# A two-layer encoder trunk: 128x128 turns of activations moved from TensorE to VectorE's 32x32 block transpose

## The chip, the cores and the metric

One core of one Trainium2 chip. The metric is the device time of one execution in microseconds (us), as the median of several executions on one chip.

## The reference

An encoder of two layers over 256 tokens of width 2048, all in float32. Each layer does

```
h    = RMSNorm(x)
u    = h @ w_in                       # q, k, v and a gate path z of four attention branches; merge gates
y_n  = attention_n(q, k, v)           # A: windowed, B: 2-D neighbourhood, C: three dilated groups, D: dense
br_n = (y_n * silu(z_n)) @ w_branch_n
m    = sum_n sigmoid(gates_n + gate_b) * br_n
x    = x + m @ w_out
```

and a last RMSNorm closes the trunk. Each branch has 4 query heads of 128.

## The kernel before, in words

**Weights.** All weights stream through the core once, as 640 tiles of 128x1024 float32 (512 KB each), called subs here and numbered j. For accuracy a sub is split in two: ScalarE rounds it to `whi` (L276), VectorE takes the rest, `wlo` = `raw` - `whi` (L277); both lines stand in the helper `halves`. TensorE multiplies the activations' own pair of halves with them, three products for each (L207 to L209 in `mm3`), 12 matmuls of 512 columns for a sub. `raw`, `whi` and `wlo` have four buffers each (`wpool`, L92); `split_w(j + 2)` is written two subs ahead (L693).

**Units.** `unit_list` (L43) sets the order of a layer: units of 8 subs that make 512 columns for all 256 tokens. M units are projections (ck, cv, cq0, cq1, cq2, cz, then akdk, avdv, aq, az, dq, dz, bk, bv, bq, bz), G units merge gates (8 subs), each followed by an R unit (2 subs, the branch's projection), P units the output projection. The order of units is fixed by hand; within an engine the order of instructions is what the tile framework's scheduler makes of it.

**What stands between units.** When a unit's last matmul is done, its 256x512 result lies in PSUM with tokens on partitions. `ev_M` (L304) applies the norm's factor and the rotary angles (`rope`, VectorE, L266 and L271) or the SiLU gate (L318, L319) into the tile `u`. Attention and the next product need features on partitions, so each 512 columns have to be turned: `turn` (L291) turns head by head with TensorE, 128x128 at a time against an identity matrix into PSUM (L299), four turns to a piece; `copy` (L338) or `split` (L346) then moves the piece to SBUF by ScalarE, or by ScalarE and VectorE as halves. `post` is the list of such pieces: one is taken from it after each sub (L704). `ev_branch` (L542) does the same for the merged gates `m` (L559), `ev_out` (L568) for the residual stream `xm`, which becomes the next layer's `h`. `k_pair` (L356) splits the keys of A and D. Attention itself (`attn_slots`, L394) is cut into slots that are spread over the subs behind a branch's z unit (L731).

```
 299   nc.tensor.transpose(tp[:, c, blk * P:(blk + 1) * P], u[:, blk, h * HD:(h + 1) * HD], ident)
 302   post.extend([lambda: None] * 2 + [lambda i=i: f(i) for i in range(n // 2)])
 693   split_w(j + LS)
 701   mm_m(outs[:1] if half else outs, hi, lo, sh, sl, 2 * si, nk, j == 0)
 704   for f in post[:1]:
 705       f()
```

Of the kernel before, what the change touches and what calls it, by code (L numbers as in the profile page):

```python
# [17 lines left out]
P = 128  # L18
SEQ = 256
D = 2048  # L20
# [62 lines left out]
def encoder_kernel(ctx: ExitStack, tc: tile.TileContext, a: dict, out: bass.AP):  # L83
# [17 lines left out]
    def nm(s):  # L101
        uid[0] += 1
        return f"{s}_{uid[0]}"
# [17 lines left out]
    def split_w(j):  # L121
        if j < NSUB:
            raw = raw_q.pop(j)
            hi = wpool.tile([P, 1024], F32R, tag="whi", name=nm("whi"))
            lo = wpool.tile([P, 1024], F32R, tag="wlo", name=nm("wlo"))
            for c in (slice(0, 512), slice(512, 1024)) if j == 0 else (slice(0, 1024),):
                halves(raw[:, c], hi[:, c], lo[:, c])
            wstate[j] = (hi, lo)
# [66 lines left out]

    hs = {}

    def h_split(layer, kt, x):
        t = per.tile([P, 2, SEQ], F32R, tag=f"h{kt}", name=nm("h"))
        g = g_sb[:, layer, kt:kt + 1] if layer else x0[:, kt:kt + 1]  # L200
        halves(x, t[:, 0, :], t[:, 1, :], g)
        hs[kt] = t


    def mm3(o, ah, al, bh, bl, start, stop):
# [24 lines left out]
    def layer_stats(layer, ss):  # L230

        t = sm.tile([P, 2, 2], F32, tag="ssp", name=nm("ssp"))
        v = sm.tile([P, 2], F32, tag="ssv", name=nm("ssv"))
        nc.vector.tensor_tensor(t, ss[:, :, 0:2], ss[:, :, 2:4], op=ALU.add)
        nc.vector.tensor_tensor(v, t[:, :, 0], t[:, :, 1], op=ALU.add)
        nc.vector.tensor_scalar(v, v, 1.0 / D, EPS, ALU.mult, ALU.add)
        S["rc"] = rsqrt(v, 2, "x")
        ev = sm.tile([P, 2], F32, tag="ev", name=nm("ev"))
        nc.vector.tensor_scalar(ev, v, EPS, None, ALU.mult)
        S["ev"] = ev  # L240

    def d_tables(layer, w):

# [44 lines left out]
    def vview(t):  # L288
        return t.rearrange("p a b -> p (a b)").rearrange("p (k m) -> p k m", k=2)

    def turn(u, n, take, post):  # L291


        def f(i):
            tp = ps_tp.tile([P, 2, SEQ], F32, tag="tp", name=nm("tu"))
            for c in range(2):
                for blk in range(2):
                    h = 2 * i + c
                    nc.tensor.transpose(tp[:, c, blk * P:(blk + 1) * P], u[:, blk, h * HD:(h + 1) * HD], ident)  # L299
            take(i, tp)  # L300

        post.extend([lambda: None] * 2 + [lambda i=i: f(i) for i in range(n // 2)])

    def ev_M(layer, name, ps, post):  # L304
        rc = [S["rc"][:, blk:blk + 1] for blk in range(2)]
        x, kind = name[0].upper(), name[1]
        if kind == "v":
            ev_v(ps, {"avdv": "avdv", "bv": "Bv", "cv": "Cv"}[name])
            if x == "B":
                b_mask()  # L310
            return
        u = wk.tile([P, 2, 512], F32, tag="u", name=nm("u"), bufs=1)
        key = x + name[1:]
        for blk in range(2):
            p, o = ps[:, blk, :], u[:, blk, :]
            if kind == "z":
                s = wk.tile([P, 512], F32, tag="t2", name=nm("zs"))
                nc.scalar.activation(s, p, AF.Sigmoid, scale=rc[blk])  # L318
                nc.vector.scalar_tensor_tensor(o, p, rc[blk], s, op0=ALU.mult, op1=ALU.mult)  # L319
            elif x == "B":  # L320
                nc.scalar.activation(o, p, AF.Copy, scale=rc[blk])
            elif x == "C" or name == "aq":
                rope(p, o, blk, cos1, sin1, rc[blk])
            elif name == "akdk":
                rope(p[:, 0:256], o[:, 0:256], blk, cos1, sin1, rc[blk])
                d_squares(p[:, 256:512], 4, blk)
                if blk == 0:
                    S["dku"] = per.tile([P, 2, 256], F32, tag="dku", name=nm("dku"))
                rope(p[:, 256:512], S["dku"][:, blk, :], blk, *S["dt"])
            else:  # L330
                d_squares(p, 0, blk)
                rope(p, o, blk, *S["dt"])
        if name == "akdk":
            turn(u, 2, lambda i, tp: k_pair("A", tp), post)
        elif x == "C" or kind == "z":
            S[key] = st()

            def copy(i, tp):  # L338
                nc.scalar.activation(S[key][:, 2 * i:2 * i + 2, :], tp, AF.Copy,
                                     **({"scale": SCALE} if kind == "q" else {}))  # L340

            turn(u, 4, copy, post)
        else:
            S[key + "h"], S[key + "l"] = st(F32R), st(F32R)

            def split(i, tp):  # L346
                two = slice(2 * i, 2 * i + 2)
                halves(tp, S[key + "h"][:, two, :], S[key + "l"][:, two, :],
                       SCALE if kind == "q" and x != "D" else None)

            if x == "D":
                d_norms()
                turn(S["dku"], 2, lambda i, tp: k_pair("D", tp), post)
            turn(u, 4, split, post)

    def k_pair(x, u):  # L356

        t = st(F32R)
        halves(u, t[:, 0:2, :], t[:, 2:4, :])
        S[x + "kh"], S[x + "kl"] = t[:, 0:2, :], t[:, 2:4, :]  # L360

    def d_squares(p, c, blk):

# [178 lines left out]
    def ev_branch(x, n, ps, post):  # L542
        G = S.pop("G")
        if x == "C":
            S[f"m{n}"] = per.tile([P, 2, 512], F32, tag=f"m{n}", name=nm("m"))
        m = S[f"m{n}"]
        for blk in range(2):
            o = m if x == "C" else G
            nc.vector.tensor_tensor(o[:, blk, :], ps[:, blk, :], G[:, blk, :], op=ALU.mult)  # L549
        if x != "C":  # L550
            nc.vector.tensor_tensor(m, m, G, op=ALU.add)  # L551
        if x == "B":

            def tr(k0):
                def f():
                    tp = ps_tp.tile([P, 2, SEQ], F32, tag="tp", name=nm("mt"))
                    for k in range(2):
                        for blk in range(2):
                            nc.tensor.transpose(tp[:, k, blk * P:(blk + 1) * P],  # L559
                                                m[:, blk, (k0 + k) * P:(k0 + k + 1) * P], ident)  # L560
                    t = st(F32R).rearrange("p (k h) t -> p k h t", k=2)
                    S[f"mt{(4 * n + k0) // 2}"] = t
                    halves(tp, t[:, :, 0, :], t[:, :, 1, :])
                return f
            post.append(tr(0))
            post.append(tr(2))

    def ev_out(n, ps, post):  # L568

        nc.vector.tensor_tensor(xm[n], ps, xm[n], op=ALU.add)  # L570
        for blk in range(2):
            s = squares(F["ss"], n, blk)
        if n == 0:
            sqrt_table(s[:, 0:1])

        def take(i, tp):
            for c in range(2):
                h_split(1, 4 * n + 2 * i + c, tp[:, c, :])

        turn(xm[n], 4, take, post)  # L580

    F = {}

# [54 lines left out]
            squares(F["ss"], n, blk)  # L638

    new_sums()  # L640
    h_tiles(0)
    split_w(0)
    split_w(1)
# [4 lines left out]
             **{8 + n: lambda n=n: first_squares(n) for n in range(4)}}  # L648
    side = []
    post = []  # L650
    last4 = []
    held = []
    j = 0
    for layer in range(DEPTH):
# [3 lines left out]
        for ui, si in sub_list(layer):  # L658
# [3 lines left out]
            if si == 0:  # L662
# [15 lines left out]
                if kind == "R":  # L678
                    yh, yl = S[name + "yh"], S[name + "yl"]
                    sh, sl = (lambda k: yh[:, k, :]), (lambda k: yl[:, k, :])  # L680
                elif kind == "P":
                    sh, sl = (lambda k, h=h: S[f"mt{k // 2}"][:, k % 2, h, :] for h in range(2))
                else:
                    sh, sl = (lambda k, h=h: hs[k][:, h, :] for h in range(2))
                opened[ui] = ps, outs, sh, sl
            ps, outs, sh, sl = opened[ui]
            nk = 2 * nsub
# [9 lines left out]
                layer_stats(0, F["ss"])  # L697
                ev_M(*held.pop())
            hi, lo = wstate.pop(j)
            half = alone and si >= 4  # L700
            mm_m(outs[:1] if half else outs, hi, lo, sh, sl, 2 * si, nk, j == 0)
            if half:
                last4.append((hi, lo, si))
            for f in post[:1]:  # L704
                f()
            del post[:1]
            if si == nsub - 1:
                if kind == "M" and "rc" not in S:
                    held.append((layer, name, ps, post))
                elif kind == "M":  # L710
                    ev_M(layer, name, ps, post)
                elif kind == "G":
                    ev_gate(layer, name, i, ps)
                elif kind == "R":
                    ev_branch(name, i, ps, post)
                elif not final:
                    ev_out(i, ps, post)
                    if i == 3:
                        layer_stats(1, F["ss"])
                else:  # L720
                    ev_last(i, 0, outs[0][1])
                    for h, l, s in last4:
# [133 lines left out]
```

## Time and profile before

| what | value |
|---|---|
| device time, median of 3 | 1867.07 us (1866.35 to 1867.41) |
| profiled execution, its own time | 1866.87 us |
| its span | 1865.1 us (1.8 us lie around it) |
| granted TensorE clock, mean | 0.999 |
| TensorE matmul busy | 1855.1 us, 99% |
| VectorE busy | 1155.6 us, 62% |
| ScalarE busy | 914.8 us, 49% |
| bytes moved by DMA | 356.95 MB, mean 191 GB/s |

The profiled execution stands 0.2 us under the median. Busy time is the time in which at least one instruction of the engine runs. A matmul's duration in the trace includes the part in which the next one already runs, so the step from one matmul's start to the next's (0.227 us for 512 columns) is what counts, not its mean duration.

### The profile page before, as it was taken

How to read it: one execution, taken by the hardware profiler on the slowest of the kernel's cores; microseconds unless marked ns; L12 is line 12 of the kernel's file. 1: busy time of each engine (PE TensorE's matmuls, PEld its weight loads, DVE VectorE, ACT ScalarE, POOL GpSimd, SP SyncE). 2: the span in 40 equal slices, each digit the busy share in tenths (PEclk: the TensorE clock that was granted, in tenths of full speed). 3: DMA queues.
4: the chain of work that ended last, by engine and by line, in shares of the span. 5: the costliest groups of instructions: out<-in, count | busy, mean ns of one | idle time of the engine just before them, and what ended most of it. 6: DMA issues, size and time to landing. Idle time of an engine off the chain costs nothing.

```text
span 1865.1 us, 22697 instructions
## 1 busy us (share of the span) xinstructions
PE 1855.1 (99%) x8560; PEld 1540.4 (83%) x8560; DVE 1155.6 (62%) x1576; ACT 914.8 (49%) x1120; POOL 0.2 (0%) x4
## 2 busy tenths in 40 slices
PE   9999999999999999999999999999999999999998
PEld 7888888888888888888888888888888888888886
DVE  7567675567654755655565576755765547556654
ACT  6445474465444644444544454744654446444443
POOL 0000000000000000000000000000000000000000
PEclk9999999999999999999999999999999999999999
DMA  9655556655765566655555555566567665666654
GB/s 327 195 188 166 170 171 196 203 169 185 219 205 187 159 199 206 200 194 188 185 187 191 182 165 170 173 197 204 174 187 214 201 189 161 204 201 194 219 190 138
DMA packets 110846, 356.95 MB, mean 191 GB/s; under 512 B 19984, under 2 KB 20496, under 8 KB 110736
## 3 DMA queue, kind: packets, MB, share of 16 engines
q1 hardware_dynamic: 110448, 354.98, 59.9%
q8 instruction: 67, 1.10, 0.2%
q10 hardware_dynamic: 288, 0.52, 0.1%
q14 instruction: 43, 0.35, 0.1%
HBM read 353.36 MB, written 2.10 MB: 191 GB/s over the span
## 4 chain that ended last, share of the span: by engine, by line
PE 99%; DMA 0%; DVE 0%; ACT 0%; issue 0%; DVEq 0%; SPq 0%
PE ps L207 31%; PE ps L209 31%; PE ps L208 31%; PE tu L299 1%; PE tp L474 1%; PE mt L559 0%; PE y L209 0%; PE y L207 0%; PE y L208 0%; PE sc L405 0%; PE sc L209 0%; PE sc L208 0%; PE sc L207 0%; PE ps L219 0%; DMA raw<-w 0%; PE sc L407 0%
## 5 line engine op out<-in xcount | busy, mean ns | idle before, releaser
L277 DVE TENSOR_TENSOR wlo<-raw,whi 128x1024 fp32r<-128x1024 f32 (+1 forms) x641 | 782.8, 1222 | 588.9 <-ACT whi L276 586.6
L276 ACT ACTIVATE whi<-raw 128x1024 fp32r<-128x1024 f32 (+1 forms) x641 | 678.4, 1059 | 819.5 <-PE ps L209 765.3
L207 PE MATMUL ps<-whi,h 128*128 128x512 f32 x2044 | 801.9, 392 | 0.0
L209 PE MATMUL ps<-whi,h 128*128 128x512 f32 x2044 | 797.4, 390 | 0.0
L208 PE MATMUL ps<-wlo,h 128*128 128x512 f32 x2044 | 796.7, 390 | 0.0
L209 PEld LDWEIGHTS ps<-whi,h 128*128 128x128 f32 x2044 | 383.7, 188 | 81.0
L208 PEld LDWEIGHTS ps<-wlo,h 128*128 128x128 f32 x2044 | 384.2, 188 | 76.3 <-DVE wlo L277 0.5
L207 PEld LDWEIGHTS ps<-whi,h 128*128 128x128 f32 x2044 | 384.1, 188 | 75.8
L207 PE MATMUL ps<-whi,st 128*128 128x512 f32 x512 | 200.5, 392 | 0.0
L209 PE MATMUL ps<-whi,st 128*128 128x512 f32 x512 | 199.6, 390 | 0.0
L208 PE MATMUL ps<-wlo,st 128*128 128x512 f32 x512 | 199.4, 389 | 0.0
L209 PEld LDWEIGHTS ps<-whi,st 128*128 128x128 f32 x512 | 96.1, 188 | 20.1
L208 PEld LDWEIGHTS ps<-wlo,st 128*128 128x128 f32 x512 | 96.2, 188 | 19.4
L207 PEld LDWEIGHTS ps<-whi,st 128*128 128x128 f32 x512 | 96.2, 188 | 19.4 <-DVE xm L598 0.2
L537 DVE SCALAR_TENSOR_TENSOR G<-ps,ry,gb 128x512 f32<-128x512 f32 x64 | 45.1, 745 | 10.5 <-PE ps L209 10.5
L447 ACT ACTIVATE p<-p,ng 128x256 f32<-128x256 f32 (+1 forms) x48 | 27.7, 578 | 36.9 <-DVE ng L446 28.9
L539 ACT ACTIVATE G<-G 128x1024 f32<-128x1024 f32 x32 | 34.0, 1062 | 10.0 <-DVE G L537 9.9
L549 DVE TENSOR_TENSOR G<-ps,G 128x512 f32<-128x512 f32 x48 | 30.9, 686 | 8.0 <-PE ps L209 8.0
L299 PE MATMUL tu<-tab,u 128*128 128x128 f32 x200 | 30.1, 271 | 0.0
L299 PEld LDWEIGHTS tu<-tab,u 128*128 128x128 f32 x200 | 24.8, 139 | 6.4
L551 DVE TENSOR_TENSOR m<-m,G 128x1024 f32<-128x1024 f32 x24 | 29.2, 1217 | 0.0
L474 PE MATMUL tp<-tab,p 128*128 128x128 f32 x128 | 24.3, 271 | 0.0
(131 smaller groups left out, 790.7 us busy)
## 6 DMA issues: line engine op xcount, KB each, us to landing
raw<-w SPq DMA_DIRECT2D x639, 512.0 KB, 3.8
gb<-gate_b SPq DMA_DIRECT2D x32, 256.0 KB, 4.3
xm<-xm SPq DMA_DIRECT2D x4, 512.0 KB, 8.4
st<-rpb SPq DMA_DIRECT2D x32, 64.0 KB, 4.5
st<-x SPq DMA_DIRECT2D x7, 256.0 KB, 7.1
dx<-tabx SPq DMA_DIRECT2D x4, 256.0 KB, 4.5
st<-fg SPq DMA_DIRECT2D x2, 512.0 KB, 5.3
out<-xm SPq DMA_DIRECT2D x4, 256.0 KB, 2.6
```

Of the source, the lines that this page charges most:

```text
L207: nc.tensor.matmul(o, ah, bh, start=start, stop=False)
L208: nc.tensor.matmul(o, ah, bl, start=False, stop=False)
L209: nc.tensor.matmul(o, al, bh, start=False, stop=stop)
L276: nc.scalar.activation(hi, u, AF.Copy)
L277: nc.vector.tensor_tensor(lo, u, f32(hi), op=ALU.subtract)
L299: nc.tensor.transpose(tp[:, c, blk * P:(blk + 1) * P], u[:, blk, h * HD:(h + 1) * HD], ident)
L447: nc.scalar.activation(p[:, 0:n], p[:, 0:n], AF.Exp, bias=ng, scale=1.0, accum_out=den)
L474: nc.tensor.transpose(H[h][:, k, blk * P:(blk + 1) * P], it["p"][:, k * P:(k + 1) * P], ident)
L537: nc.vector.scalar_tensor_tensor(G[:, blk, :], ps[:, blk, :], S["rc"][:, blk:blk + 1], gb, op0=ALU.mult, op1=ALU.add)
L539: nc.scalar.activation(G, G, AF.Sigmoid)
L549: nc.vector.tensor_tensor(o[:, blk, :], ps[:, blk, :], G[:, blk, :], op=ALU.mult)
L551: nc.vector.tensor_tensor(m, m, G, op=ALU.add)
```

## The change

`turn` now uses VectorE's transpose, which turns blocks of 32x32, for all that TensorE turned before, except the attention weights (L474), which stay on TensorE. One instruction takes 32 partitions `a` to `a+32` and writes them, turned, to partitions `c` to `c+32`, 8 blocks (4 heads, 2 token blocks) of 32 columns at once; 16 of them turn 512 columns, 16 with 4 blocks the 256 columns of a key tile. `post` takes four instructions at a time. Tiles that are wanted whole are written to their place directly (no copy by ScalarE; the scale of the queries is folded into the factor `rcq`); tiles that are wanted as halves go to one buffer `T` and are split from there in one piece of 1024 columns. `whi` and `wlo` have three buffers instead of four, and the last unit's final three subs, not four, are held for its second half.

```
-            hi = wpool.tile([P, 1024], F32R, tag="whi", name=nm("whi"))
-            lo = wpool.tile([P, 1024], F32R, tag="wlo", name=nm("wlo"))
+            hi = wpool.tile([P, 1024], F32R, tag="whi", name=nm("whi"), bufs=3)
+            lo = wpool.tile([P, 1024], F32R, tag="wlo", name=nm("wlo"), bufs=3)
...
+        S["rcq"] = sm.tile([P, 2], F32, tag="rcq", name=nm("rcq"))
+        nc.vector.tensor_scalar(S["rcq"], S["rc"], SCALE, None, ALU.mult)
...
-    def turn(u, n, take, post):
-
-
-        def f(i):
-            tp = ps_tp.tile([P, 2, SEQ], F32, tag="tp", name=nm("tu"))
-            for c in range(2):
-                for blk in range(2):
-                    h = 2 * i + c
-                    nc.tensor.transpose(tp[:, c, blk * P:(blk + 1) * P], u[:, blk, h * HD:(h + 1) * HD], ident)
-            take(i, tp)
-
-        post.extend([lambda: None] * 2 + [lambda i=i: f(i) for i in range(n // 2)])
+    def turn(u, dst, post, done=None):
+
+        x = u.rearrange("p b (h d) -> p h b d", d=HD)
+        y = dst.rearrange("p h (b t) -> p h b t", b=2)
+
+        def f(c):
+            for a in range(0, P, 32):
+                nc.vector.transpose(y[c:c + 32, :, :, a:a + 32], x[a:a + 32, :, :, c:c + 32])
+            if c == 96 and done:
+                done()
+
+        post.extend(lambda c=c: f(c) for c in range(0, P, 32))
...
+    def turned(n=4):
+        return wk.tile([P, 4, SEQ], F32, tag="T", name=nm("T"), bufs=1)[:, 0:n, :]
+
+    def turn_split(u, hi, lo, post):
+        t = turned(hi.shape[1])
+        turn(u, t, post, lambda: halves(t, hi, lo))
...
-            half = alone and si >= 4
+            half = alone and si >= 5
```

Where the turns now stand on VectorE is the scheduler's doing. The first place is the stretch behind a projection of branch C, here unit cq0 of the first layer: `ps` is its result, `u` the rotated tile, `st` the turned one, `wlo` the low halves of the weights that the following subs need. Before, VectorE had there:

```order
L271 TENSOR_TENSOR u_697<-u_697,t_134_698 128x512
L277 TENSOR_TENSOR wlo_732<-raw_679,whi_731 128x1024
L266 SCALAR_TENSOR_TENSOR t_135_703<-ps_552,ry_430,tab 128x4x64 x2
L277 TENSOR_TENSOR wlo_750<-raw_710,whi_749 128x1024
L271 TENSOR_TENSOR u_697<-u_697,t_135_703 128x512
L277 TENSOR_TENSOR wlo_774<-raw_729,whi_773 128x1024
L277 TENSOR_TENSOR wlo_798<-raw_747,whi_797 128x1024
L277 TENSOR_TENSOR wlo_816<-raw_771,whi_815 128x1024
```

and now:

```order
L276 TENSOR_TENSOR u_689<-u_689,t_119_690 128x512
L282 TENSOR_TENSOR wlo_705<-raw_653,whi_704 128x1024
L271 SCALAR_TENSOR_TENSOR t_120_695<-ps_544,rcq_424,tab 128x4x64 x2
L282 TENSOR_TENSOR wlo_728<-raw_671,whi_727 128x1024
L276 TENSOR_TENSOR u_689<-u_689,t_120_695 128x512
L282 TENSOR_TENSOR wlo_750<-raw_702,whi_749 128x1024
L303 STREAM_TRANSPOSE st_700<-u_689 32x8x32 x12
L282 TENSOR_TENSOR wlo_772<-raw_725,whi_771 128x1024
L303 STREAM_TRANSPOSE st_700<-u_689 32x8x32 x4
L282 TENSOR_TENSOR wlo_794<-raw_747,whi_793 128x1024
```

Twelve transposes in a row now stand between two low halves, and four more before the next.

The second place is unit dz and the start of the gate unit behind it, where D's keys (`dku`) and queries are turned through `T` and split (`st`), the gate path is made (`u`) and D's attention begins (`mx`):

```order
L282 TENSOR_TENSOR wlo_3406<-raw_3357,whi_3405 128x1024
L303 STREAM_TRANSPOSE T_3310<-dku_1445 32x4x32 x16
L282 TENSOR_TENSOR wlo_3428<-raw_3379,whi_3427 128x1024
L282 TENSOR_TENSOR st_3309<-T_3310,st_3309 128x512
L282 TENSOR_TENSOR wlo_3450<-raw_3403,whi_3449 128x1024
L303 STREAM_TRANSPOSE T_3311<-u_3275 32x8x32 x12
L282 TENSOR_TENSOR wlo_3472<-raw_3425,whi_3471 128x1024
L303 STREAM_TRANSPOSE T_3311<-u_3275 32x8x32 x4
L282 TENSOR_TENSOR wlo_3511<-raw_3447,whi_3510 128x1024
L324 SCALAR_TENSOR_TENSOR u_3493<-ps_3312,ry_416,zs_3494 128x512
L282 TENSOR_TENSOR st_3293<-T_3311,st_3292 128x1024
L324 SCALAR_TENSOR_TENSOR u_3493<-ps_3312,ry_416,zs_3497 128x512
```

There were only splits of the turned tiles at this place before; now the turns themselves stand there, 16 small and 16 large ones.

## Rows read from the trace of the kernel before

**Rows 1.** The page: busy time of the engines, and the chain that ended last.
```profile
PE 1855.1 (99%) x8560; PEld 1540.4 (83%) x8560; DVE 1155.6 (62%) x1576; ACT 914.8 (49%) x1120; POOL 0.2 (0%) x4
...
PE 99%; DMA 0%; DVE 0%; ACT 0%; issue 0%; DVEq 0%; SPq 0%
```
**Rows 2.** Groups by form, TensorE's turns: count, busy us, mean ns, idle before.
```profile
L299 PE MATMUL tu<-tab,u 128*128 128x128 f32 x200 | 30.1, 271 | 0.0
L559 PE MATMUL mt<-tab,m 128*128 128x128 f32 x64 | 9.8, 276 | 0.1
L299 PE MATMUL tu<-tab,xm 128*128 128x128 f32 x32 | 4.8, 272 | 0.0
L299 PE MATMUL tu<-tab,dku 128*128 128x128 f32 x8 | 1.5, 272 | 0.0
```
**Rows 3.** Timeline, ScalarE, steady stretch of branch C: start us, us, what, idle before.
```profile
94.56 1.06 ACT L276 ACTIVATE whi<-raw 128x1024 fp32r<-128x1024 f32 x1 [1.66 <-PE ps L209]
97.28 1.06 ACT L276 ACTIVATE whi<-raw 128x1024 fp32r<-128x1024 f32 x1 [1.66 <-PE ps L209]
100.00 1.06 ACT L276 ACTIVATE whi<-raw 128x1024 fp32r<-128x1024 f32 x1 [1.66 <-PE ps L209]
```
**Rows 4.** Windows of single units: us, then busy us (count) of each engine.
```profile
74.36:97.09 22.73, 22.73 (x106) 18.80 (x105) 13.80 (x16) 9.47 (x10) 0.00 (x0) 1.00 0.58 186
170.09:197.57 27.48, 27.48 (x142) 23.09 (x141) 22.83 (x58) 13.66 (x24) 0.00 (x0) 1.00 0.48 153
221.29:244.39 23.10, 23.10 (x110) 19.16 (x109) 15.14 (x20) 10.80 (x13) 0.00 (x0) 1.00 0.58 182
383.33:406.92 23.59, 23.59 (x113) 19.53 (x112) 18.06 (x32) 14.07 (x17) 0.00 (x0) 1.00 0.58 182
406.92:435.07 28.15, 28.15 (x152) 23.86 (x151) 20.84 (x47) 21.02 (x35) 0.00 (x0) 1.00 0.50 156
757.79:780.57 22.78, 22.78 (x106) 18.73 (x105) 13.34 (x13) 9.57 (x10) 0.00 (x0) 1.00 0.60 203
```
**Rows 5.** Timeline, VectorE, the same stretch: the rotary part of cq1 between low halves.
```profile
95.65 1.23 DVE L277 TENSOR_TENSOR wlo<-raw,whi 128x1024 fp32r<-128x1024 f32 x1 [1.50 <-ACT whi L276]
97.28 0.75 DVE L266 SCALAR_TENSOR_TENSOR u<-ps,ry,tab 128x512 f32<-128x512 f32 x1 [0.40 <-PE ps L209]
...
99.99 1.22 DVE L277 TENSOR_TENSOR wlo<-raw,whi 128x1024 fp32r<-128x1024 f32 x1
101.12 0.87 DVE L266 SCALAR_TENSOR_TENSOR t<-ps,ry,tab 128x256 f32<-128x256 f32 x2
101.91 1.22 DVE L277 TENSOR_TENSOR wlo<-raw,whi 128x1024 fp32r<-128x1024 f32 x1
103.04 0.68 DVE L271 TENSOR_TENSOR u<-u,t 128x512 f32<-128x512 f32 x1
103.82 1.23 DVE L277 TENSOR_TENSOR wlo<-raw,whi 128x1024 fp32r<-128x1024 f32 x1
```
**Rows 6.** Timeline, TensorE: first matmuls of two subs that use Rows 5's halves.
```profile
97.08 0.39 PE L207 MATMUL ps<-whi,h 128*128 128x512 f32 x1
...
102.52 0.39 PE L207 MATMUL ps<-whi,h 128*128 128x512 f32 x1
```
**Rows 7.** Groups by form, VectorE's nearest operations: count, busy us, mean ns.
```profile
L466 DVE TENSOR_SCALAR p<-p,rd 128x256 f32<-128x256 f32 x64 | 22.5, 352 | 1.7
L271 DVE TENSOR_TENSOR u<-u,t 128x512 f32<-128x512 f32 x24 | 16.4, 682 | 0.0
L277 DVE TENSOR_TENSOR st<-yz,st 128x256 fp32r<-128x256 f32 x32 | 13.4, 420 | 3.0 <-ACT st L276 2.3
L462 DVE TENSOR_TENSOR p<-p 128x128 f32<-128x128 f32 x16 | 4.6, 290 | 9.9 <-ACT p L447 9.9
```
**Rows 8.** Timeline, VectorE: two instructions, the second using the first's result.
```profile
257.36 0.15 DVE L459 TENSOR_TENSOR den<-den,es 128x1 f32<-128x1 f32 x1
257.55 0.16 DVE L465 RECIPROCAL rd<-den 128x1 f32<-128x1 f32 x1
```

More of the change, by code (lines that the diff above doesn't have):

```diff
@@ L196, in encoder_kernel, with h_tile @@
     hs = {}
+    def h_tile(n):
+        hs[n] = per.tile([P, 2, 4, SEQ], F32R, tag=f"h{n}", name=nm("h"))
+        return hs[n]
     def h_split(layer, kt, x):
-        t = per.tile([P, 2, SEQ], F32R, tag=f"h{kt}", name=nm("h"))
+        t = hs[kt // 4][:, :, kt % 4, :]
         g = g_sb[:, layer, kt:kt + 1] if layer else x0[:, kt:kt + 1]
         halves(x, t[:, 0, :], t[:, 1, :], g)
-        hs[kt] = t
     def mm3(o, ah, al, bh, bl, start, stop):
@@ L289, in vview @@
         return t.rearrange("p a b -> p (a b)").rearrange("p (k m) -> p k m", k=2)
-    def turn(u, n, take, post):
-        def f(i):
-            tp = ps_tp.tile([P, 2, SEQ], F32, tag="tp", name=nm("tu"))
-            for c in range(2):
-                for blk in range(2):
-                    h = 2 * i + c
-                    nc.tensor.transpose(tp[:, c, blk * P:(blk + 1) * P], u[:, blk, h * HD:(h + 1) * HD], ident)
-            take(i, tp)
-        post.extend([lambda: None] * 2 + [lambda i=i: f(i) for i in range(n // 2)])
+    def turn(u, dst, post, done=None):
[7 more added lines that the diff above has]
+        post.extend(lambda c=c: f(c) for c in range(0, P, 32))
     def ev_M(layer, name, ps, post):
-        rc = [S["rc"][:, blk:blk + 1] for blk in range(2)]
+        rc = [S["rcq" if name[1] == "q" and name[0] != "d" else "rc"][:, blk:blk + 1] for blk in range(2)]
         x, kind = name[0].upper(), name[1]
@@ L333, in ev_M, with k_pair @@
         if name == "akdk":
-            turn(u, 2, lambda i, tp: k_pair("A", tp), post)
+            k_pair("A", u[:, :, 0:256], post)
         elif x == "C" or kind == "z":
             S[key] = st()
[L338 to L342, printed above, removed]
+            turn(u, S[key], post)
         else:
             S[key + "h"], S[key + "l"] = st(F32R), st(F32R)
[L346 to L349, printed above, removed]
             if x == "D":
                 d_norms()
-                turn(S["dku"], 2, lambda i, tp: k_pair("D", tp), post)
-            turn(u, 4, split, post)
-    def k_pair(x, u):
+                k_pair("D", S["dku"], post)
+            turn_split(u, S[key + "h"], S[key + "l"], post)
+    def turned(n=4):
[3 more added lines that the diff above has]
+        turn(u, t, post, lambda: halves(t, hi, lo))
+    def k_pair(x, u, post):
         t = st(F32R)
-        halves(u, t[:, 0:2, :], t[:, 2:4, :])
         S[x + "kh"], S[x + "kl"] = t[:, 0:2, :], t[:, 2:4, :]
+        turn_split(u, S[x + "kh"], S[x + "kl"], post)
     def d_squares(p, c, blk):
@@ L552, in ev_branch @@
         if x == "B":
[L554 to L566, printed above, removed]
+            S[f"mh{n}"], S[f"ml{n}"] = st(F32R), st(F32R)
+            turn_split(m, S[f"mh{n}"], S[f"ml{n}"], post)
     def ev_out(n, ps, post):
@@ L574, in ev_out, with split @@
             sqrt_table(s[:, 0:1])
[L576 to L580, printed above, removed]
+        h_tile(n)
+        t = turned()
+        def split():
+            for c in range(4):
+                h_split(1, 4 * n + c, t[:, c, :])
+        turn(xm[n], t, post, split)
     F = {}
@@ L640, in encoder_kernel @@
     new_sums()
+    for n in range(4):
+        h_tile(n)
     h_tiles(0)
@@ L650, in encoder_kernel @@
     post = []
-    last4 = []
+    late = []
     held = []
@@ L681, in encoder_kernel @@
                 elif kind == "P":
-                    sh, sl = (lambda k, h=h: S[f"mt{k // 2}"][:, k % 2, h, :] for h in range(2))
+                    sh, sl = (lambda k, h=h: S[f"m{h}{k // 4}"][:, k % 4, :] for h in "hl")
                 else:
-                    sh, sl = (lambda k, h=h: hs[k][:, h, :] for h in range(2))
+                    sh, sl = (lambda k, h=h: hs[k // 4][:, h, k % 4, :] for h in range(2))
                 opened[ui] = ps, outs, sh, sl
@@ L699, in encoder_kernel @@
             hi, lo = wstate.pop(j)
-            half = alone and si >= 4
+            half = alone and si >= 5
             mm_m(outs[:1] if half else outs, hi, lo, sh, sl, 2 * si, nk, j == 0)
             if half:
-                last4.append((hi, lo, si))
+                late.append((hi, lo, si))
             for f in post[:1]:
@@ L721, in encoder_kernel @@
                     ev_last(i, 0, outs[0][1])
-                    for h, l, s in last4:
+                    for h, l, s in late:
                         mm_m(outs[1:], h, l, sh, sl, 2 * s, nk)
```

## The prediction

> **What bounds the kernel now.** I read the page first: TensorE is busy 99% of the span, and the chain that ended last is TensorE's to 99% [rows 1]. So a microsecond taken from TensorE's own work is a microsecond of the whole, and work on VectorE (62% busy) costs only where TensorE comes to wait for it. Next I asked for the groups by form, to count TensorE's turns [rows 2], then for windows of single units, to see what is free on VectorE beside each [rows 4], and for the timelines of one stretch of branch C, to see how far VectorE runs ahead of TensorE [rows 3, 5, 6].
>
> The reader is to see a chain of buffers. ScalarE's rounding of each sub waits until TensorE gives a `whi` buffer back [rows 3]; it comes every 2.72 us, which is one sub. VectorE's low half follows. The low half that ends at 96.88 [rows 5] is used by the sub that starts at 102.52 [rows 6]: it lies 5.64 us ahead. That lead is what VectorE may be late by before TensorE has to wait.
>
> **What the change takes from TensorE.** Rows 2 count 200 + 64 + 32 + 8 = 304 turns, 76 groups of four. A steady unit of eight subs takes 8 x 2.72 = 21.76 us; the first window of rows 4 has two groups in it and takes 22.73. So a group costs 0.97 / 2 = 0.485 us, and 76 of them 36.9 us, all on the path. This is the whole gain; ScalarE's copies that go away were beside TensorE and are counted at nothing.
>
> **What it puts on VectorE.** 36 turns of 16 instructions with 256 columns each (576) and 4 turns of 16 with 128 columns (64). No row shows such an instruction. The nearest are VectorE's operations of the same number of float32 columns between SBUF tiles: 420 ns for 256 columns, 290 ns for 128 [rows 7]. Two instructions that need nothing of each other overlap: in rows 5 the one behind the low half starts at 101.12, though that half ends at 101.21, which is 0.09 us earlier; where the second uses the first's result it starts 0.04 us after the end [rows 8]. So a step of 0.33 us is one end (0.42 - 0.09); below it nothing speaks for a gain, since the transpose has no second input to save. The other end is 0.68 us, the 512-column row of rows 7, if a 4-byte column counts twice. I take **0.46 us** (0.42 + 0.04; for small ones 0.29 + 0.04 = 0.33), because each of these instructions reads other partitions than the one ahead of it, which no overlapping pair of rows 5 does, so I count no overlap.
>
> Beside that row stands a rule. The Trainium skill, "VectorE: DVE Perf Modes", section "Two Vector instructions with no wait between them", says that an instruction which starts in another group of 32 partitions than the last one read or wrote is held until all before it have finished. By that rule the overlap of rows 5 is lost in all 640, and the sum belongs near my value and not near the 0.33 end; no run here shows it yet. The same page, "The three transpose paths", gives 311 ns for 128 bf16 columns; an estimate from it, with 130 ns for 128 more columns by rows 7, is 0.44 us, by which the sum below would be about 1862.
>
> The splits that remain get a little cheaper (one of 1024 columns for two of 512), 0.15 us a turn; I leave that out.
>
> **What the third buffer does.** With three buffers instead of four, a `whi` buffer comes free one sub later, so the lead is at most 5.64 - 2.72 = 2.92 us. In each sub, 2.72 us less the low half's step of 1.13 (99.99 to 101.12, rows 5) leaves 1.59 us for all else; what VectorE does beyond that is taken from the lead, and what goes below zero is time in which TensorE waits.
>
> **Where TensorE then waits**, place by place:
>
> - Branch C's rotated units (three in the first layer, four in the second). The rotary part takes 2.71, 0.79 and 0.78 us between low halves [rows 5], so the lead goes 2.92, 1.80, 2.60, 2.92. Then twelve turns, 5.52 us: 2.92 + 1.59 - 5.52 = -1.01; then four, 1.84: -0.25. That is 1.26 us a unit, 7 units, 8.8 us.
> - The very first unit's 16 turns stand in one run: 2.92 + 1.59 - 7.36 = -2.9 us, once.
> - Unit az, with the turn of A's queries in runs of eight, four and four, the first beside a rotary add and two small operations of 1.3 us in all: 2.60 + 1.59 - 5.0 = -0.8, then twice -0.25. 1.3 us a layer, 2.6.
> - Unit avdv, behind A's and D's keys: VectorE 22.83 + 16 x 0.33 = 28.1 us of work for TensorE's 27.48 - 0.49 = 27.0 [rows 4]; 1.1 us a layer, 2.2.
> - Unit dz and D's first gate unit: VectorE is busy 18.06 + 20.84 = 38.9 us there [rows 4], and gets 16 small and 32 large turns, 5.3 + 14.7: 58.9 us. TensorE needs 23.59 + 28.15 less five groups, 49.3. Of the 9.6 us too much the lead covers 2.92: 6.7 a layer, 13.4 us.
> - All other turns stand by four or six between low halves: 1.84 us against 1.59, four times, which the lead covers. The merged gates' window shows the room: 13.34 + 7.36 = 20.7 us of work in 21.8 [rows 4].
>
> Together 29.9 us. For what these tallies leave out (the scores of D that wait for its queries, the last merged block and the last input block, which TensorE needs within six subs of the layer's turn, ScalarE's rounding that comes late behind a table load) I allow 8 us, an estimate between 0 and 15, since with 2.92 us each of them counts sooner.
>
> **The sum.** 1866.87 - 36.9 + 29.9 + 8 = 1867.9, so **1868 us**; the profiled execution stands 0.2 us under the median, which I neglect. Gain and loss cancel. The one number that decides is the step: 112 turns in C's units, 16 in the first, 96 in D's stretch and 64 around A add up to 288 that stand where nothing covers them, so 10 ns of step are 2.9 us of time.
>
> **The rivals.**
>
> *VectorE overlaps the turns (faster).* If blocks from other partitions step like the pairs of rows 5, at 0.33 us (0.20 for small ones), twelve of them take 3.96 us, under the 4.51 that lead and sub give, and TensorE does not wait in C's units. The first run loses 0.8, D's stretch 38.9 + 3.2 + 10.6 - 49.3 - 2.92 = 0.5 a layer; with half the allowance, 1866.9 - 36.9 + 1.8 + 4 = 1836 us. For it: all independent pairs of rows 5 overlap. Against it: none of them changes partitions. At 0.40 us it is still about 1852. Chance 0.30.
>
> *A 4-byte transpose is slower than an add (slower).* At 0.68 us TensorE waits 3.65 + 1.13 = 4.8 us in a C unit (33 in seven), the first run 6.4, az 4.8 a layer, avdv 2.5, D's stretch 15.2, and the 22 or so turns that were covered lose 4 x 1.13 less the lead, 1.6 each: about 120 us in all, 1960. The point from which it decides is 0.50 us, where the sum is about 1880. VectorE is then the bound in every projection: 13.80 + 16 x 0.68 = 24.7 us of work in C's 21.76 [rows 4]. For it: no row prices this operation, and it moves data across partitions, which none of rows 7 does. Against it: no row either has a float32 column counted twice. Chance 0.22.
>
> That the change does not do what it says is no case: in its order all 640 instructions stand on VectorE and the 304 are gone from TensorE.
>
> **How the numbers follow.** The forecast is the case of a step from 0.43 to 0.50 us, chance 0.48, with a range of its own of 1859 to 1880. The range that is to hold 8 times in 10 goes from the first rival's 1836 to 1910 (a step of 0.57 us, on the line from 1880 at 0.50 to 1960 at 0.68) and leaves out about 0.05 below and 0.12 above. A measurement of this kernel can tell 0.2%, 3.7 us, from no change. The first rival is faster as a whole (0.30); of the forecast's 0.48, 0.07 is faster, 0.21 within 0.2% and 0.20 slower; the second rival is slower (0.22). So faster 0.37, same 0.21, slower 0.42.
>
> **What would show it.** In the changed kernel's profile: the transposes' mean and the step between two of a run, near 0.42 and 0.46; TensorE's turns gone but its share of the span under 99%; waits of TensorE for VectorE's low half (L282), none of which show now, about 30 us, in C's units at the sub after the run of twelve and in D's first gate unit; low halves that end 2.9 us ahead of their sub where VectorE has room. The prediction is wrong in its main step if the run of twelve takes under 4.5 us or over 6.5, or if TensorE waits at places without turns.

## The result, and the profile after

The changed kernel takes 1876.6 us (median of 5, 1874.5 to 1879.2) against 1867.07 us (1866.35 to 1867.49) before: a ratio of 1.0051, 95% interval 1.004 to 1.0063. It is slower by half a per cent. The profiled execution is the longest of the five, 1879.2 us, with a span of 1877.4.

The page after, with the lines that answer to [rows 1]:

```profile
PE 1839.2 (98%) x8256; PEld 1512.2 (81%) x8256; DVE 1406.4 (75%) x2202; ACT 895.6 (48%) x1072; POOL 0.2 (0%) x4
...
PE 80%; DVE 15%; issue 3%; ACT 1%; DMA 0%; SPq 0%; DVEq 0%; ACTq 0%
```

The 304 turns are gone from TensorE (8560 matmuls, now 8256), VectorE went from 62% to 75%, and the chain that ended last, TensorE's to 99% before, is VectorE's to 15%. What TensorE waits for, the three largest (line, releaser, us in total, times, longest):

```profile
PE ps L211 <- DVE wlo L282: 17.8, 21, 2.5
PE tp L475 <- DVE yz L497: 5.7, 4, 2.3
PE tp L475 <- DVE p L467: 2.0, 2, 1.0
```

The transposes, two of their forms (count, busy us, mean ns):

```profile
L303 DVE STREAM_TRANSPOSE st<-u 32x256 f32<-32x256 f32 x256 | 111.6, 436 | 3.9
L303 DVE STREAM_TRANSPOSE T<-dku 32x128 f32<-32x128 f32 x32 | 9.7, 303 | 0.4
```

The stretch of branch C that [rows 5] show, one unit later, on VectorE (start us, us, what):

```profile
103.23 1.22 DVE L282 TENSOR_TENSOR wlo<-raw,whi 128x1024 fp32r<-128x1024 f32 x1
104.37 0.87 DVE L271 SCALAR_TENSOR_TENSOR t<-ps,rcq,tab 128x256 f32<-128x256 f32 x2
105.16 1.21 DVE L282 TENSOR_TENSOR wlo<-raw,whi 128x1024 fp32r<-128x1024 f32 x1
106.29 0.68 DVE L276 TENSOR_TENSOR u<-u,t 128x512 f32<-128x512 f32 x1
107.06 1.23 DVE L282 TENSOR_TENSOR wlo<-raw,whi 128x1024 fp32r<-128x1024 f32 x1
108.20 5.37 DVE L303 STREAM_TRANSPOSE st<-u 32x256 f32<-32x256 f32 x12
113.60 1.22 DVE L282 TENSOR_TENSOR wlo<-raw,whi 128x1024 fp32r<-128x1024 f32 x1
```

The run of twelve takes 5.37 us, 0.448 a step. The low half behind it ends at 114.82; TensorE had begun that sub at 113.92 and stands still:

```profile
113.92 0.39 PE L210 MATMUL ps<-whi,h 128*128 128x512 f32 x1
114.88 0.50 PE L211 MATMUL ps<-wlo,h 128*128 128x512 f32 x1 [0.57 <-DVE wlo L282]
115.22 0.40 PE L212 MATMUL ps<-whi,h 128*128 128x512 f32 x1
```

The windows of units that answer to [rows 4], in the same order (cq2 stands for the unit of C; the column behind POOL is the granted clock):

```profile
100.09:123.12 23.03, 22.39 (x97) 17.86 (x96) 20.51 (x33) 8.49 (x8) 0.00 (x0) 1.00 0.55 178
172.73:203.64 30.91, 28.77 (x138) 23.94 (x137) 28.27 (x76) 13.95 (x23) 0.00 (x0) 0.94 0.43 138
227.36:250.62 23.26, 23.03 (x102) 18.15 (x101) 22.03 (x35) 10.86 (x11) 0.00 (x0) 1.00 0.51 163
389.54:412.10 22.56, 22.27 (x97) 17.86 (x96) 20.95 (x48) 12.58 (x14) 0.00 (x0) 1.00 0.49 163
412.10:448.02 35.92, 30.87 (x145) 24.11 (x144) 34.22 (x74) 18.06 (x31) 0.00 (x0) 0.95 0.42 136
770.32:792.08 21.76, 21.76 (x97) 18.02 (x96) 20.11 (x29) 9.34 (x9) 0.00 (x0) 1.00 0.58 192
```

The merged gates' unit is 1.02 us shorter, the whole gain of its two groups. The unit of C is 0.30 longer, unit avdv 3.4, and D's first gate unit 7.8. In avdv and in that gate unit the granted clock is 0.94 and 0.95: TensorE's clock fell there.

To see where the time went I took the start of each sub's first matmul in both traces, took 0.121 us (0.485 / 4) for each turn off the subs of before that held one, and summed the differences by unit. In us, both layers, over TensorE's time without any turn (the last column is 0.121 times the number of turns by construction, and the columns of kernels hold what was lost in their profiled executions):

| place | forecast | changed kernel | four buffers | best kernel | before, with its turns |
|---|---|---|---|---|---|
| first units, ck to cq0 | 2.9 | 4.4 | 1.3 | 1.8 | 1.0 |
| C's seven other units | 8.8 | 8.7 | 0.2 | 0.2 | 6.8 |
| avdv | 2.2 | 8.0 | 4.2 | 1.0 | 1.0 |
| az | 2.6 | 2.2 | 0.0 | 0.1 | 1.9 |
| dz and D's first gate unit | 13.4 | 18.3 | 13.8 | 4.8 | 4.8 |
| gate units behind az and bz, all else | 8 | 7.9 | 8.6 | 4.3 | 21.3 |
| sum | 37.9 | 49.5 | 28.1 | 12.2 | 36.8 |

"Four buffers" and "best kernel" are runs told of below (E5 and E10). D's first gate unit is, as in the prediction, the one behind dz (its gates are A's); beside the gate units behind az, dz and bz run the attentions of A, D and B, and beside akdk, avdv and aq that of C.

### The profile page after: what moved, and what is told of

The parts are those of the page before. It is cut to its first block, busy times and chain, and to the rows that moved or that the text cites. A ratio compares the mean times of both kernels' runs of the same rounds, so it can differ in the third digit from the quotient of the medians.

```text
span 1877.4 us, 22632 instructions
## 1 busy us (share of the span) xinstructions
PE 1839.2 (98%) x8256; PEld 1512.2 (81%) x8256; DVE 1406.4 (75%) x2202; ACT 895.6 (48%) x1072; POOL 0.2 (0%) x4
## 3 DMA queue, kind: packets, MB, share of 16 engines
q1 hardware_dynamic: 110448, 354.98, 58.5%
## 4 chain that ended last, share of the span: by engine, by line
PE 80%; DVE 15%; issue 3%; ACT 1%; DMA 0%; SPq 0%; DVEq 0%; ACTq 0%
PE ps L211 26%; PE ps L212 26%; PE ps L210 26%; DVE wlo L282 5%; DVE st L303 5%; DVE T L303 3%; ACT whi L281 1%; PE tp L475 1%; PE y L211 0%; PE y L212 0%; PE y L210 0%; DMA raw<-w 0%; DVE t L271 0%; DVE u L324 0%; PE sc L210 0%
## 5 line engine op out<-in xcount | busy, mean ns | idle before, releaser
L211 PE MATMUL ps<-wlo,h 128*128 128x512 f32 x2044 | 803.5, 393 | 18.6 <-DVE wlo L282 17.8
L303 DVE STREAM_TRANSPOSE st<-u 32x256 f32<-32x256 f32 x256 | 111.6, 436 | 3.9
L303 DVE STREAM_TRANSPOSE T<-u 32x256 f32<-32x256 f32 (+1 forms) x160 | 65.5, 409 | 9.3 <-ACT u L326 6.8
L303 DVE STREAM_TRANSPOSE T<-m 32x256 f32<-32x256 f32 x128 | 55.8, 436 | 2.3
L281 ACT ACTIVATE st<-T 128x1024 fp32r<-128x1024 f32 (+1 forms) x20 | 19.5, 975 | 49.7 <-DVE T L303 49.7
```

Of the source, the lines that this page charges most:

```text
L211: nc.tensor.matmul(o, ah, bl, start=False, stop=False)
L281: nc.scalar.activation(hi, u, AF.Copy)
L303: nc.vector.transpose(y[c:c + 32, :, :, a:a + 32], x[a:a + 32, :, :, c:c + 32])
```

## The experiments

The theory after the comparison: TensorE's gain is as forecast, and is lost again where a run of turns on VectorE is longer than the lead of the low halves (2.92 us with three buffers) and TensorE has to wait; at the longest waits the clock falls too. Its rivals: the third buffer costs by itself; or VectorE's sum of work is the bound, wherever the turns stand and however many buffers there are. E2 and E3 ask about the step of a transpose. All kernels compute the whole reference. In those with `PE = (...)`, the tiles named there are turned by TensorE with the code of before, the rest by VectorE.

### E1: three buffers alone

```
-            hi = wpool.tile([P, 1024], F32R, tag="whi", name=nm("whi"))
+            hi = wpool.tile([P, 1024], F32R, tag="whi", name=nm("whi"), bufs=3)
...
-            half = alone and si >= 4
+            half = alone and si >= 5
```

(`wlo` as `whi`.)

> The kernel before, with one part of the change alone: three whi and wlo buffers instead of four, and the last unit's cut at the fifth sub. All 304 turns stay on TensorE. Theory (the third buffer costs nothing by itself; it only cuts the lead that VectorE's turns then use up): low halves end 2.92 us ahead of their sub instead of 5.64, VectorE's longest stretch between two low halves (the rope, 2.71 us in it) still fits 2.92 + 1.59, so TensorE does not wait: 1867 to 1870 us, no fall of the granted clock. Rival (the shorter lead alone makes TensorE wait, whoever does the turns): 1877 us or more, with waits of TensorE for wlo in the units of branch C.

1866.73 us, ratio 1.0001 (0.9992 to 1.0011). TensorE's waits for low halves in the whole span:

```profile
PE ps L208 <- DVE wlo L277: 0.8, 1, 0.8
```

The lead is 2.92 us in 252 subs, where before has 5.64 in 206, and that costs nothing as long as VectorE has no long runs. The rival that the third buffer costs by itself falls.

### E2: each transpose in two

```
-                nc.vector.transpose(y[c:c + 32, :, :, a:a + 32], x[a:a + 32, :, :, c:c + 32])
+                for b in range(2):
+                    nc.vector.transpose(y[c:c + 32, :, b, a:a + 32], x[a:a + 32, :, b, c:c + 32])
```

> The changed kernel with each transpose of 256 columns cut into two of 128 columns, one behind the other, the second with the same 32 source and the same 32 destination partitions as the first. Theory (two transposes do not overlap because the second starts in other partitions than the first read or wrote; where the second writes the first's partitions but reads others, as here, that does not change): a step of 0.303 + 0.01 for each, 0.63 us a pair against 0.448, a run of twelve pairs 7.5 us, about 1930 us. Rival (with the same source and destination partitions the second overlaps): a step inside a pair of about 0.22, 0.53 a pair, a run of twelve 6.4 us, about 1900 us.

1901.4 us in its one execution: the rival. One entry of `post`, now eight half transposes, between two low halves, and the group by form:

```profile
89.92 2.03 DVE L306 STREAM_TRANSPOSE st<-u 32x128 f32<-32x128 f32 x8
...
L306 DVE STREAM_TRANSPOSE st<-u 32x128 f32<-32x128 f32 x512 | 130.2, 284 | 4.9
```

Eight times 284 ns is 2.27 us, and they take 2.03: 0.06 us of overlap for each of the four pairs. In the single records the second of a pair starts 0.235 us after the first, which lasts 0.302; the next pair, which reads other partitions, starts 0.013 us after the end of the one ahead. So transposes do overlap, by 0.067 us, when they read the same 32 partitions and write the same 32 as the one ahead, also where the two groups of 32 differ from each other.

### E3: the loops of a turn exchanged

```
-        def f(c):
-            for a in range(0, P, 32):
+        def f(a):
+            for c in range(0, P, 32):
```

> The changed kernel with the two loops of a turn exchanged: four transposes one behind the other now read the same 32 partitions and write four different ones, where before they read four and wrote the same. Theory (a change of the partitions that are read ends the overlap, a change of those that are written does not): three of four steps fall from 0.448 to about 0.37 us, the run of twelve from 5.37 to 4.7, TensorE's waits in C's units from 1.2 to about 0.4: 1855 to 1866 us. Rival (a change of either ends it): steps of 0.448, 1874 to 1880 us, as the changed kernel.

1877.37 us, ratio 1.0058 (1.0041 to 1.0074), as the changed kernel: the rival. The run of twelve:

```profile
107.41 5.37 DVE L305 STREAM_TRANSPOSE st<-u 32x256 f32<-32x256 f32 x12
```

Now the source stays and the destination changes, and the run takes the same 5.37 us. A change of either ends the overlap. Since the 16 transposes of a turn differ in one or the other, 0.448 us is what they take.

### E4: four buffers again, with three for `raw`

```
-            t = wpool.tile([P, 1024], F32, tag="raw", name=nm("raw"))
+            t = wpool.tile([P, 1024], F32, tag="raw", name=nm("raw"), bufs=3)
-            hi = wpool.tile([P, 1024], F32R, tag="whi", name=nm("whi"), bufs=3)
+            hi = wpool.tile([P, 1024], F32R, tag="whi", name=nm("whi"), bufs=4)
```

(`wlo` as `whi`; loads are issued three subs ahead instead of four.)

> The changed kernel with all turns on VectorE, but four whi and wlo buffers again (and three raw buffers instead of four, which makes the room in SBUF; the cut of the last unit at the fourth sub as before). Theory (the loss is the lead of 2.92 us that the runs of turns use up): with a lead of 5.64 the run of twelve (5.37 us) fits 5.64 + 1.59, so C's units and the first unit wait for nothing; what is left is D's stretch, about 10 us of waits for wlo in two layers, about 5 to 10 us at A's and D's attention, and at most two falls of the clock at 1.7 us: 1866.9 - 36.9 + 11 + 8 = 1849, 1845 to 1856 us. Rival (VectorE's sum of work bounds, buffers do not matter): 1870 us or more, with waits for wlo about as many as in the changed kernel.

1881.96 us, ratio 1.008 (1.0065 to 1.0095). By its time it is the rival's, and TensorE's waits for low halves (19.1 us, 14 of them) are as large as in the changed kernel; but the reason is neither's. ScalarE's waits, of this kernel and then of the changed one, and what the loads of this one wait for:

```profile
ACT whi L283 <- PE ps L214: 490.9, 322, 4.1
ACT whi L283 <- DMA raw<-w: 276.2, 161, 6.8
```

```profile
ACT whi L281 <- PE ps L212: 724.9, 460, 3.1
```

```profile
SPq L120 <- DVE wlo L284: 1380.8, 584, 8.9
```

ScalarE now waits for loads, 276 us in all. A `raw` buffer comes free when VectorE has made the low half (584 of the 639 loads wait for one), so with three of them a late VectorE makes the load late as well. The experiment traded one lead for another and does not decide between the two; E5 does.

### E5: four buffers, and four for `raw`

The room comes from `T`, which shares the gates' buffer `G`:

```
-        return wk.tile([P, 4, SEQ], F32, tag="T", name=nm("T"), bufs=1)[:, 0:n, :]
+        return wk.tile([P, 4, SEQ], F32, tag="G", name=nm("T"), bufs=1)[:, 0:n, :]
```

(`whi` and `wlo` have four buffers as in E4, and the last unit is cut at its fourth sub again.)

> The changed kernel with all turns on VectorE and four whi and wlo buffers, with all four raw buffers kept: the room comes from the tile T, which shares one buffer with the gates' tile G. Theory (the loss is the lead of 2.92 us; the run with three raw buffers was spoiled by late loads, 276 us of ScalarE's waits for them): low halves end up to 5.64 us ahead of their sub, C's units and the first unit wait for nothing, D's stretch about 10 us in two layers, A's and D's attention 5 to 10 us, the clock falls at most twice at 1.7 us: 1849, 1845 to 1856 us. Rival (VectorE's work bounds, the buffers do not matter): 1870 us or more, with waits for wlo in C's units of 1.2 us each as in the changed kernel.

1859.4 us, ratio 0.9963 (0.9948 to 0.9978). VectorE in branch C, and TensorE's waits for low halves in the whole span:

```profile
103.73 7.18 DVE L305 STREAM_TRANSPOSE st<-u 32x256 f32<-32x256 f32 x16
110.94 4.63 DVE L284 TENSOR_TENSOR wlo<-raw,whi 128x1024 fp32r<-128x1024 f32 x4
...
PE ps L213 <- DVE wlo L284: 2.4, 5, 0.8
```

Even a run of sixteen now costs nothing, with nothing to spare: the lead falls from 5.64 us to 0.01, four low halves follow at once, and C's units lose 0.2 us where they lost 8.7. So the lead is what decided in C, and VectorE's sum does not. But 1859.4 is 10 us over the middle of the theory and past its range, and what is left is not in C: the table's third column has 13.8 us in D's stretch, and 8.6 in the last row, of which 5.2 stand behind az (2.0 in the changed kernel). E8 and E9 ask what they are.

### E6: D's keys and queries back on TensorE, three buffers

```
+    PE = ('Dk', 'Dq')
```

> The changed kernel with three buffers, but D's keys and queries turned by TensorE as before (3 groups of four turns a layer go back, 48 VectorE instructions a layer leave). Theory (in the stretch of unit dz and D's first gate unit VectorE has more work than TensorE): the waits there, 18.3 us in two layers, go down to nearly nothing, TensorE gets 6 x 0.485 = 2.9 us back, and the falls of the clock at D's first gate unit (2 x 1.7 us, in the 18.3) go too: 1876.6 - 18.3 + 2.9 = 1861, 1858 to 1865 us. Waits in C's units stay at 1.2 us each. Rival (the waits at D come from the attention's own chain and only move on): 1872 us or more.

1863.29 us, ratio 0.998 (0.997 to 0.9989), inside the theory's range. The units dz and D's first gate unit fall from 18.3 us over TensorE's own time to 5.0; C's units keep their 1.23 to 1.28 us each.

### E7 and E8: less on VectorE, four buffers

E7 keeps D's keys and queries on TensorE, E8 all of C's, A's and D's keys and queries:

```
+    PE = ('Dk', 'Dq')
...
+    PE = ('Ck', 'Cq0', 'Cq1', 'Cq2', 'Ak', 'Dk', 'Aq', 'Dq')
```

> As the run before it (four whi and wlo buffers, T beside G), but D's keys and queries turned by TensorE, 6 groups of four turns in all. Theory: 70 groups off TensorE give 70 x 0.485 = 34 us; the waits for wlo in D's stretch go, about 5 us at the attention remain, no fall of the clock: 1866.9 - 34 + 1 + 6 = 1840, 1836 to 1846 us. Rival (what VectorE has too much only moves to the next place without cover): 1850 us or more.

> Four whi and wlo buffers, T beside G, and VectorE turns only what stands where it has room (the merged gates, the second layer's input and B's heads, with A's z: 48 groups); C's heads, A's and D's keys and queries stay on TensorE, 28 groups. Theory: 48 x 0.485 = 23.3 us come off TensorE and nothing waits: 1866.9 - 23.3 + 1 = 1845, 1843 to 1849 us; so the run that moves 22 groups more is faster by about 5 us only if their waits are as small as told. Rival (transposes on VectorE cost also where they fit between low halves): 1852 us or more.

E7 1856.27 us, ratio 0.9945 (0.993 to 0.996); E8 1856.55 us, 0.9948 (0.9933 to 0.9963). Both stand on their rivals' side, 16 and 12 us over the theory. By the table's method E7 still loses 7.7 us in D's stretch and 7.9 in avdv, where the clock falls once a layer. In E8 the excess is in the gate units behind a z, in each layer 2.6 us behind az (two units), 2.4 behind dz and 1.4 behind bz, where before's two groups of turns cost 0.97 each. There VectorE has 16 transposes more between the steps of an attention's softmax, and TensorE waits for those:

```profile
PE tp L495 <- DVE p L487: 2.6, 4, 0.7
PE tp L495 <- DVE yz L517: 1.7, 2, 0.9
```

### E9: the z heads of A, D and B on TensorE too

```
+    PE = ('Ck', 'Cq0', 'Cq1', 'Cq2', 'Ak', 'Dk', 'Aq', 'Dq', 'Az', 'Dz', 'Bz')
```

> The run with 48 groups on VectorE and four buffers, but the z heads of A, D and B turned by TensorE again (12 groups go back, 36 stay on VectorE). Theory (beside an attention VectorE has no room even with the lead of 5.64: the first gate units behind a z cost 2.6, 2.4 and 1.4 us over what their own work takes, where TensorE's two groups of turns cost 0.97): 2 x (1.65 + 1.45 + 0.4) = 7 us less than that run's 1856.5: 1849.5, 1847 to 1852 us. Rival (the 2.6, 2.4 and 1.4 come from something else than the z heads, such as T and G in one buffer): 1860 us or more, since 12 groups go back to TensorE for nothing.

1849.66 us, ratio 0.991 (0.9895 to 0.9925). Twelve groups went back to TensorE and the kernel got 7 us faster. The table's method gives 0.91 to 0.97 for each of the three gate units, so `T` beside `G` is not what cost there.

### E10 and E11: C's turns on VectorE again, with four and with three buffers

```
+    PE = ('Ak', 'Dk', 'Dq', 'Az', 'Dz', 'Bz')
```

> Four buffers, T beside G, and on VectorE only what stands outside the attentions: C's heads, A's and B's queries, B's keys, merged gates, second layer's input (56 groups); A's and D's keys, D's queries and the three z heads stay on TensorE (20 groups). Theory: the run with the z heads on TensorE, less 20 groups (C's heads, A's queries) x 0.485 = 9.7 us, plus about 0.6 us of wait at the first unit's sixteen turns and 0.03 in each other C unit: 1840.5, 1838 to 1844 us, no fall of the clock. Rival (C's turns cost in the lead of what follows): 1847 us or more.

> The same 56 groups on VectorE and 20 on TensorE as in the run of 1841.5 us, but with the changed kernel's three whi and wlo buffers and T in its own buffer. Theory (at a lead of 2.92 us only C's units, the first unit and unit az lose): 1841.5 + 7 x 1.23 + 2.5 at the first unit + 1.7 for a fall of the clock behind it + 2 x 1.1 in unit az = 1856.5, 1853 to 1859 us. Rival (with A's, D's and B's turns on TensorE the smaller lead does no harm): 1845 us or less.

E10 1841.48 us, ratio 0.9864 (0.985 to 0.9877): it beats both kernels, by 25 and 35 us. E11 1855.63 us, 0.9943 (0.9927 to 0.996). Both lie inside their theories' ranges. So of the 35 us between the changed kernel and E10, 14 are the fourth buffer and 21 the place of the turns; taken in the other order, by E5, 17 are the buffer and 18 the place. E10's page:

```profile
PE 1827.5 (99%) x8336; PEld 1516.9 (82%) x8336; DVE 1338.5 (73%) x2012; ACT 902.6 (49%) x1086; POOL 0.2 (0%) x4
...
PE 96%; DVE 2%; issue 1%; DMA 0%; ACT 0%; SPq 0%; DVEq 0%
```

VectorE is busy 73%, nearly as much as the changed kernel's 75%, and the chain is TensorE's again. Together with E5, where VectorE is busy 76% and the kernel is 7 us faster than before, this also settles the rival of VectorE's sum.

### E12: matmuls of zeros in three of the long waits

```
+            if (name, i, si) in (("cq0", 0, 1), ("A", 0, 1)) and kind in "MG" and (kind == "G" or layer == 0):
+                for k in range(8):
+                    nc.tensor.matmul(outs[0][1], z, hs[0][:, 0, 0:2, :], start=False, stop=False)
```

The zeros `z` leave the sums as they are.

> The changed kernel with eight more matmuls of zeros added into the open sum (1.8 us each time) ahead of three subs: the second of cq0 in the first layer and the second of A's first gate unit in both layers, where TensorE waits 2.5 to 2.9 us for a low half and the granted clock then fell. The low half comes when it comes, so the eight matmuls lie inside the wait. Theory (the falls follow TensorE's idle stretch): the three falls there go, the two at A's attention stay: 3 x 1.7 = 5.1 us less, 1871.5, 1870 to 1874 us. Rival (the falls have another cause, or the matmuls push what follows): 1876 us or more.

1876.67 us, ratio 1.0056 (1.0043 to 1.0069): by its time the rival. Its windows behind the first of the three places and behind the second:

```profile
56.90:60.30 3.40, 3.23 (x14) 2.65 (x15) 3.40 (x5) 1.00 (x2) 0.00 (x0) 1.00 0.54 173
...
419.90:423.50 3.60, 3.60 (x13) 3.02 (x13) 2.63 (x4) 0.69 (x1) 0.00 (x0) 0.55 0.40 146
```

In cq0 the fall is gone, and the unit's excess goes from 4.26 to 2.71 us. In D's gate units the wait was only moved: TensorE now waits 2.2 us a layer for D's queries in the scores instead,

```profile
PE sc L212 <- ACT st L283: 4.4, 2, 2.2
```

and the clock falls behind that. The stretch from D's first key transpose to the start of its last four z transposes takes 32.3 us in both kernels, and VectorE is busy in 30.7 of them in the changed kernel: VectorE sets its length, and what TensorE saves inside it is waited for later. (The two falls that the expectation puts at A's attention stand in avdv, beside C's.) So the reason given for the falls stands where the wait was really filled, once; that is one unit of one run, and the 1.6 us are less than the five executions scatter (1875.65 to 1878.6).

## Why the prediction came out as it did

The forecast was 1868, no change, the measurement 1876.6, half a per cent slower; the range, and the case taken as likeliest (a step from 0.43 to 0.50 us, 1859 to 1880), hold it. By its own steps:

- **The gain of 36.9 us was right.** Where the changed kernel waits for nothing, a unit with two groups falls by all of it (bv, 22.73 to 21.76; merged gates, 22.78 to 21.76), and E9, with 36 groups on VectorE and hardly a wait, gains 17.1 us where 36 x 0.485 are 17.5.
- **The step was right.** 0.46 was taken, 0.448 measured, and both rivals, at 0.33 and 0.68, are out. The reason for it, that each instruction reads other partitions than the one ahead, held too. By the Trainium skill, "VectorE: DVE Perf Modes", section "Two Vector instructions with no wait between them", an instruction is held if its input starts in another group of 32 partitions than the last input did, or its output in another than the last output; E2 (0.235 us in a pair with both the same, 0.302 + 0.013 otherwise) and E3 (0.448 us with the source the same) agree with both halves of it.
- **The lead was right**: 2.92 us where VectorE has room (209 subs have just this), and C's seven units lose 8.7 us against 8.8. E1 and E5 show that it takes both, fewer buffers and long runs. Unit az came to 2.2 (2.6).
- **The allowance of 8 us** for what the tallies leave out came to 7.9, but that is luck: of the places that it names, the last merged block shows 0.9 us and the last input block nothing, D's scores fall into D's stretch, and 7.2 us stand in the gate units behind az and bz, beside attentions, which it does not name.
- **What failed is the term "29.9 us" of waits, by 11.7** in the profiled execution, the longest of the five (for the median the whole sum is 8.7 short). Of these 8.5 are a mechanism that the prediction did not have: TensorE's granted clock fell five times in the profiled execution, behind its waits in the first layer's cq0 and, in both layers, avdv and D's first gate unit; each fall is a stretch of 3.4 us at half speed, 1.7 us. Next, avdv was tallied as VectorE's work less TensorE's time, 2.2 (the lead, which is taken off in D's stretch, was not; it would have left nothing), where 4.6 were lost besides the clock: there TensorE doesn't wait for a low half (the lead never goes under 1 us) but for `yz` of C's attention (2.1 and 2.3 us; `tp` and `y` share two PSUM buffers, L473 and L486, and VectorE's `yz` frees one), so the lead covers nothing. And D's stretch cost 1.5 us more than the 13.4, the clock apart. That it came so near is in part luck: the tally puts VectorE at 58.9 us a layer in these two units, and the windows show it busy 55.2 (20.95 + 34.22) of 58.5, so TensorE waits there for the order of VectorE's work too and not for its sum alone. The first unit (0.2 less, the clock apart), az (0.4 less) and C (0.1 less) make up the rest.
- **Of the signs**, the waits for low halves came to 17.8 us where about 30 were named; beside them stand 7.7 us of waits for `yz` and `p`, and the clock. The rest showed as told: 436 ns and 0.448 us, a share of 98%, 5.37 us for the run of twelve.

So the tally by lead is right for what waits on low halves, and can be wrong beside an attention, where a transpose delays a chain that TensorE needs before long. The same gap made the expectations of E5, E7 and E8 10 to 16 us too low, and E9, which was told from the measured excess, came out within 0.2 us.

Left open: how much of the two falls in D's stretch is a loss of its own. The 32.3 us in both kernels of E12 speak for TensorE's time inside that stretch being hidden by VectorE's, but the clock falls there in both, so this isn't shown; the five times 1.7 us are an upper bound, and what the falls there do not cost is a loss of the stretch itself.

## What to carry to other kernels

Before work is moved to an engine that is 62% busy, ask place by place what waits for that engine there and how late it may be: VectorE at 75% cost 9.5 us over before with three buffers, at 76% it gave 7 us with four (E5), and at 73%, with four buffers and another choice of turns, 25 us (E10). A buffer given up beside such a move costs nothing alone (E1) and 14 us (E10, E11) or 17 (E5) with it, so it is to be counted together with the longest run that the moved work makes. Work that stands beside a chain with steps on both engines (a softmax) can have no lead to hide behind, even when a window shows room. It need not cost: C's z, turned in akdk beside the first steps of C's attention, loses under 0.1 us a layer.

## What the runs showed that had not been expected

**TensorE's clock falls behind short waits.** The changed kernel, behind the first unit's wait and around it (window, its length, busy us of TensorE first, granted clock in the column behind POOL):

```profile
50.00:54.00 4.00, 4.00 (x19) 3.34 (x18) 3.88 (x10) 1.64 (x2) 0.00 (x0) 1.00 0.34 126
54.00:56.80 2.80, 0.42 (x2) 0.00 (x1) 2.73 (x6) 1.06 (x1) 0.00 (x0) 1.00 0.00 0
56.80:60.20 3.40, 3.40 (x8) 2.63 (x9) 3.40 (x4) 0.69 (x1) 0.00 (x0) 0.53 0.63 180
60.20:64.00 3.80, 3.80 (x18) 3.16 (x17) 1.36 (x2) 1.12 (x2) 0.00 (x0) 0.97 0.76 249
```

and TensorE's own rows there:

```profile
54.04 0.39 PE L210 MATMUL ps<-whi,h 128*128 128x512 f32 x1
56.80 0.62 PE L211 MATMUL ps<-wlo,h 128*128 128x512 f32 x1 [2.38 <-DVE wlo L282]
57.22 0.63 PE L212 MATMUL ps<-whi,h 128*128 128x512 f32 x1
57.65 0.63 PE L210 MATMUL ps<-whi,h 128*128 128x512 f32 x1
```

TensorE stood still for 2.38 us; then eight matmuls step by 0.427 us instead of 0.227, at the lower of the two levels (1.2 of 2.4 GHz), which costs 1.6 us more than the wait itself. The other four falls of this execution follow waits of 2.1 and 2.3 us (avdv) and 2.5 us (D's first gate unit); the wait of 1.6 us two subs later in that unit is followed by none. It is not the same in each execution: E12 shows no fall behind 2.2 us in the second layer's avdv, and behind a wait of 1.91 us in the first layer's avdv E7 has a fall and E5 has none. In all traces of this case 30 falls stand ahead of the kernels' ends, each beginning within a wait of 1.67 us or more or up to 1.5 us behind it, and the kernels whose longest wait is 1 us (before, E1, E8, E9, E10) have none. The mean clock of the five executions goes from 0.994 in the longest (1879.2 us) to 0.997 in the shortest (1874.5), in order of their times. Before, whose longest waits are 1 us, shows 1.00 up to the end of its last sub.

**A buffer's price is in what frees it.** Three `raw` buffers instead of four (E4) cost 22.6 us against E5, though a load lands 4.1 us after its issue (median) and three subs last 8.2 us: the buffer comes free by the engine that is late.
